# Four quarter products side by side in place of one float32 product of 128 weight columns

## The chip, the cores and the metric

The kernel runs on one core of a Trainium2 chip, as one launch. The metric is the device time of that core in microseconds. The kernel before takes 1728.89 us, the median of three runs (1727.22 to 1729.65).

## What is computed

Three layers run one after the other on 256 tokens of 1024 features, all in float32. Each layer is a mixer (products with large weights, around an attention or a recurrence) followed by a routed set of experts:

```
layer 0: forgetting attention + S5 scan    -> 16 experts of 256, two per token
layer 1: mLSTM, 8 heads of 128             -> 16 experts of 256, two per token
layer 2: sparse attention (8 heads of 128)
         + HGRN2 (8 heads of 128)
         + retention (4 heads, 256 x 512)  -> 32 experts of 512, two per token
```

Layer 2 scales and shifts its inputs by vectors worked out from a second input, `mod = silu(c) @ ada_w + ada_b`. The parts that the change touches are these:

```
s   = einsum('bhnld,bhnjd->bhnlj', qc, kc) * Dmat         # mLSTM scores; num = s @ v + ...
attn = einsum('bhtd,bhsd,bhtsd->bhts', qt, kt, decay)     # HGRN2
attn = einsum('bhtd,bhsd->bhts', qt, kt) * intra_decay    # retention; o = attn @ v + ...
logits = x @ w_group + b_group, x @ w_expert + b_expert   # both routers' kinds
```

## The kernel before, in words

Activations stand on the chip throughout. Weights come in pieces of 1 MB through a ring of tiles: `place` takes the next tile, `weights` (L246 to L261) issues the load on SP (L260). Where a list `after` is set, GpSimd first copies one value of a mark into the tile (L250), which holds the load back until an earlier piece was split; the marks are made in `split_now` (L279).

The large products of the mixers are made from halves. Each weight piece is split into a rounded part hi by ScalarE (L285) and a rest lo by VectorE (L286), and `mm3` issues three products (L301, L302, L303) of 128 weight columns and 256 streamed ones in a faster number format (float32r). These make up most of TensorE's work in the mixers. Everything else on TensorE is plain float32, which the engine does in two passes: one matmul of the program is one weight load and one product per pass, so two records of each in the trace.

Around the large products stand smaller float32 ones, and the names of their lines are used below:
- L565: the modulation for layer 2, done in small steps beside the mixers. Products with a streamed column of ones, four to each of 12 groups (4 groups in the second mixer, 8 in the third).
- L590: a vector spread over rows, with a diagonal tile as the streamed one.
- L956 to L958 (`attn_out`): scores by values, three products of 128 streamed columns to a head, for the mLSTM (sd and v), sparse attention (PT and av), HGRN2 (AT or AO and bi) and retention (AR and cv).
- L1199: the routers' logits, 8 products to each half of the tokens, 20 or 36 streamed columns; L1092 on VectorE reads them.
- L1537: scores of the mLSTM heads, an early half of 256 and a late half (t0 = 128) of 128 streamed columns.
- L1858 and L1853: HGRN2's levels. For each of seven levels in two halves VectorE makes qw (L1848), GpSimd fills in W (L1849, L1856), TensorE makes eight products of 64 streamed columns (L1858), and VectorE copies them into AT under a mask (L1861).
- L1923: retention's scores, again with an early and a late half.
- L872 and L906 belong to the S5 scan of layer 0. They are already issued with 32 weight columns at a column position of the array (`tile_position=(0, 32 * q)`), as are some of the experts' products in L1324. They are not changed.

The order of the instructions on each engine is written out ahead of the run: the framework simulates the program with its own costs and orders each engine's queue by it. A change in the number of instructions can so move others, on other engines too. Each engine works through its queue in order.

Of the kernel before, what the change touches and what calls it, by code (L numbers as in the profile page):

```python
# [200 lines left out]
class Net:  # L201
# [96 lines left out]
    def mm3(self, out, a, b, first, last):  # L298
# [3 lines left out]
        nc.tensor.matmul(out, a[0], b[1], start=False, stop=False)  # L302
        nc.tensor.matmul(out, a[1], b[0], start=False, stop=last)  # L303

    def dense_feat(self, hT, srcs, evac):


        c = 0
        q = None
        for src in srcs:  # L310
            w = self.weights(src)
            nk, n = w.shape[1], w.shape[2]
            step = min(n, 1024 // nk)
            for s0 in range(0, n, step):
                hi, lo = self.split(w[:, :, s0:s0 + step])
                for j in range(step // 128):
                    if q is None:
                        q = self.ps("z").rearrange("p (c t) -> p c t", c=2)
                    s = slice(128 * j, 128 * j + 128)
                    for k in range(nk):  # L320
                        self.mm3(q[:, c % 2, :], (hi[:, k, s], lo[:, k, s]), (hT[0][:, k, :], hT[1][:, k, :]), k == 0, k == nk - 1)
                    c += 1
                    if c % 2 == 0:
                        evac(c - 2, q)
                        q = None
        if q is not None:
            evac(c - 1, q)
# [190 lines left out]
    def v(self, name, n=128):  # L518

        at = VEC_AT[name]  # L520
        return self.vec[:n, at:at + dict(VEC)[name]]
# [23 lines left out]
    def modulation(self, p, js, every, bufs, after):  # L545


        nc, A, ct = self.nc, self.A, self.v("ct")
        def bits():
            for j in js:  # L550
                acc = p.tile([128, 512], F32, name="md")
                for k in range(8):
                    w = p.tile([128, 512], F32, name="aw", bufs=bufs)
                    if j == js[0] and k < bufs:
                        nc.gpsimd.tensor_copy(w[:, :1], after)
                    nc.sync.dma_start(w, A["aw"][j, k])
                    c = ct[:, k:k + 1]
                    if k:
                        nc.vector.scalar_tensor_tensor(acc, w, c, acc, op0=ALU.mult, op1=ALU.add)  # L559
                    else:  # L560
                        nc.vector.tensor_scalar(acc, w, c, None, op0=ALU.mult)
                    yield
                q = self.ps("a")
                for i in range(4):
                    nc.tensor.matmul(q[:, i:i + 1], acc[:, i * 128:(i + 1) * 128], self.ones[:, :1], start=True, stop=True)  # L565
                m = slice(4 * j, 4 * j + 4)
                nc.vector.tensor_add(self.modT[:, m], self.v("abT")[:, m], q[:, :4])
        self.beside, self.every, self.units = bits(), every, 0
# [12 lines left out]
    def rows(self, vec, tag):  # L581

        nc = self.nc
        out = []
        for n in range(2):
            q = self.ps(tag)
            for c in range(4):
                d = self.sm.tile([128, 128], F32, name="diag")
                nc.scalar.activation(d, self.ident, AF.Identity, scale=vec[:, 4 * n + c:4 * n + c + 1])
                nc.tensor.matmul(q[:, 128 * c:128 * c + 128], self.ones[:, :128], d, start=True, stop=True)  # L590
            out.append(q)
        return out

# [358 lines left out]

    def attn_out(self, a00, a01, a11, v, o):

        nc = self.nc
        nc.tensor.matmul(o[:, :128], v(0), a00, start=True, stop=True)  # L956
        nc.tensor.matmul(o[:, 128:256], v(0), a01, start=True, stop=False)  # L957
        nc.tensor.matmul(o[:, 128:256], v(1), a11, start=False, stop=True)  # L958

    def gate_in(self, p, hT, w, bias, name):  # L960

# [193 lines left out]
    def moe_core(self, l, x, gT, bT, add, end, po, first=None, last=None):  # L1155
# [4 lines left out]
        tc, nc, A = self.tc, self.nc, self.A  # L1160
# [13 lines left out]
        with self.phase(f"moe{l}", y=4, o=3, t=1) as p:  # L1174
            rw, rb = self.v(f"rw{l}").rearrange("p (k n) -> p k n", k=8), self.v(f"rb{l}")
# [3 lines left out]
            hT = xtile("mhT")  # L1179
            qs, rs, mr = [], [], []  # L1180
            for b in range(2):
                if l < 2:
                    mr.append(self.moments(x, b))
                    rs.append(mr[b][1])
                else:
                    rs.append(self.sm.tile([128, 1], F32, name="xrs"))
                    self.inv_rms_rows(x, b, rs[b], lambda c: hh[:, b, c * 512:(c + 1) * 512])
                for k in range(0, 8, 4):
                    v = self.ps("o").rearrange("p (k t) -> p k t", k=4)
                    for j in range(4):  # L1190
                        nc.tensor.transpose(v[:, j], x[:, b, 128 * (k + j):128 * (k + j) + 128], self.ident)
                    d = hT[:, k:k + 4, 128 * b:128 * b + 128]
                    if k:
                        nc.vector.tensor_copy(d, v)
                    else:
                        nc.scalar.activation(d, v, AF.Copy)
                qs.append(self.ps("y")[:, :rw.shape[2]])
                for k in range(8):
                    nc.tensor.matmul(qs[b], hT[:, k, 128 * b:128 * b + 128], rw[:, k, :], start=k == 0, stop=k == 7)  # L1199
            weigh, mk = self.route(p, l, ne, qs, rb, rs)  # L1200

            for b in range(2):
# [15 lines left out]
            q = self.ps("t")  # L1218
# [304 lines left out]
    def mlstm_heads(self, p, half, qT, kT, v, nm, aT):  # L1523

        nc = self.nc
        den = self.ps("n")
        num = self.late.tile([128, 4, 256], F32, name="num", bufs=2)
        r0 = 32 * half
        for i in range(4):
            hd = 4 * half + i  # L1530
            r = row_of(hd)
            d, s = self.ps("a"), self.ps("a")
            for o, t0 in ((0, 0), (256, 128)):
                n = 256 - t0
                nc.tensor.matmul(d[:, o:o + n], self.oh[:, hd, :], nm[:, t0:], start=True, stop=False)
                nc.tensor.matmul(d[:, o:o + 128], self.identb, self.cmtb, start=False, stop=True)
                nc.tensor.matmul(s[:, o:o + n], kT[:, i, t0:t0 + 128], qT[:, i, t0:], start=True, stop=True)  # L1537
            D = p.tile([128, 384], F32, name="Dm", bufs=2)
            nc.scalar.activation(D[:, :256], d[:, :256], AF.Exp, bias=aT[:, 0, r:r + 1])
            nc.scalar.activation(D[:, 256:], d[:, 256:384], AF.Exp, bias=aT[:, 1, r:r + 1])  # L1540
            sd = p.tile([128, 384], F32, name="sd", bufs=4)
            nc.vector.scalar_tensor_tensor(sd, s[:, :384], 128.0 ** -0.5, D, op0=ALU.mult, op1=ALU.mult)
            blocks = [sd[:, j * 128:(j + 1) * 128] for j in range(3)]
            o = self.ps("a")
            self.attn_out(*blocks, lambda kb: v[:, kb, i * 128:(i + 1) * 128], o[:, :256])
            nc.scalar.activation(num[:, i], o[:, :256], AF.Copy)
            m = r0 + 4
            oc = self.ones_column(r0 + i, m)
            nc.tensor.matmul(den[:m, :256], oc, sd[:, :256], start=i == 0, stop=False, skip_group_check=True)
            nc.tensor.matmul(den[:m, 128:256], oc, sd[:, 256:], start=False, stop=i == 3, skip_group_check=True)  # L1550
        return num, den
# [253 lines left out]
    def hgrn_weights(self, p, hT, half, e, lv):  # L1805

        nc = self.nc
# [26 lines left out]
        for i, m in enumerate((128, 64, 32, 16, 8, 4, 2, 1)):  # L1834
# [15 lines left out]
            s = self.ps("a")  # L1850
            if m == 128:
                for j in range(4):
                    nc.tensor.matmul(s[:, 128 * j:128 * j + 128], W[:, j, :128], qw[:, 128 * j:128 * j + 128], start=True, stop=True)  # L1853
                nc.scalar.activation(AO, s.rearrange("p (h t) -> p h t", h=4), AF.Copy)
                continue
            nc.gpsimd.tensor_copy(w1[:, :, :1], of(kk, m, 1)[:, :, :1])  # L1856
            for j in range(8):
                nc.tensor.matmul(s[:, 64 * j:64 * j + 64], W[:, j // 2, 128 * (j % 2):128 * (j % 2) + 128],  # L1858
                                 qw[:, 64 * j:64 * j + 64], start=True, stop=True)
            mk = lv[:, i - 1, :].bitcast(U16).rearrange("p (n s m) -> p n s m", s=2, m=m)[:, :, 1, :]  # L1860
            nc.vector.copy_predicated(AT.rearrange("p h b (n s m) -> p (h b) n s m", s=2, m=m)[:, :, :, 1, :],  # L1861
                                      mk.unsqueeze(1).to_broadcast([128, 8, 64 // m, m]),
# [35 lines left out]
    def retention_weights(self, p, hT, rot, half):  # L1898
# [20 lines left out]
        for h in range(2):  # L1919
            s = self.ps("a")  # L1920
            for o, t0 in ((0, 0), (256, 128)):
                for j in range(2):
                    nc.tensor.matmul(s[:, o:o + 256 - t0], ck[:, 2 * h + j, t0:t0 + 128], cq[:, 2 * h + j, t0:], start=j == 0, stop=j == 1)  # L1923
            nc.vector.tensor_tensor(AR[:, h], s[:, :384], dec[:, h], op=ALU.mult)
        return AR

# [78 lines left out]
```

## Time and profile before

| | |
|---|---|
| median of three runs | 1728.89 us |
| profiled execution | 1725.18 us |
| its span, first to last instruction | 1723.4 us |
| mean granted clock of TensorE | 0.913 |
| TensorE busy | 1491.4 us, 87% |
| VectorE / ScalarE / GpSimd busy | 851.5 / 615.5 / 258.1 us |
| HBM read | 467.56 MB |

The first mixer lies from 0 to 172 us, its experts up to 366; the second mixer from 366 to 490, its experts up to 650; the third mixer from 650 to about 1240, its experts to the end. In the profile PE is TensorE's products, PEld its weight loads, DVE VectorE, ACT ScalarE, POOL GpSimd, SP the queue that issues most transfers. The rows of stages give start and end, length, the busy time of PE, PEld, DVE, ACT and POOL with instruction counts, the granted clock, the busy share of the DMA engines and GB/s. The rows in order of time give start, length, engine, line and operation, tiles, shapes and a count where like instructions follow each other. A product's length in the profile reaches from its start to its modelled end, and products overlap; what one costs is therefore read from the distance between starts.

### The profile page before, as it was taken

The page shows a single profiled execution, that of the slowest core. Times are in us where ns is not written, and L with a number is a line of the kernel's source. Part 1 is how long each engine was busy: PE and PEld are TensorE (multiplying, and loading weights), DVE is VectorE, ACT ScalarE, POOL GpSimd, SP SyncE. Part 2 cuts the span into 40 slices and gives each one's busy share as a digit, 9 for nine tenths or more (in the row PEclk, how much of TensorE's full clock was granted, in tenths as well). Part 3 has the DMA queues.
Part 4 walks back from the last instruction along what each step waited for, and adds up shares of the span by engine and source line. Part 5 has one row for each costly group of instructions (what it writes and reads, how often), then busy time and mean ns, then how long its engine had stood idle before and what let it go on. Part 6 is the DMA issues. An engine that isn't in the chain of part 4 may idle for free.

```text
span 1723.4 us, 26173 instructions
## 1 busy us (share of the span) xinstructions
PE 1491.4 (87%) x10705; PEld 1058.6 (61%) x10705; DVE 851.5 (49%) x1411; ACT 615.5 (36%) x921; POOL 258.1 (15%) x290
## 2 busy tenths in 40 slices
PE   7889899799989978999999999999986766668664
PEld 6768544588864427999999999999830211113111
DVE  6665522677663236977887768567720000001002
ACT  4344311466531214557565455455510000002001
POOL 7840100000010001002214212225300000000000
PEclk9989999999989998999999999999987887777876
DMA  9714995665479916663464566444799999999996
GB/s 276 174 54 156 420 421 228 227 222 194 164 306 421 393 42 211 230 206 136 168 215 143 191 221 225 172 167 176 322 421 421 421 421 421 421 421 421 421 422 247
DMA packets 82266, 471.37 MB, mean 274 GB/s; under 512 B 12496, under 2 KB 14424, under 8 KB 29392
## 3 DMA queue, kind: packets, MB, share of 16 engines
q1 hardware_dynamic: 77920, 457.28, 68.2%
q0 software_dynamic: 2224, 8.85, 2.2%
q10 hardware_dynamic: 1984, 3.37, 0.8%
q8 instruction: 90, 1.47, 0.3%
q14 instruction: 48, 0.39, 0.1%
HBM read 467.56 MB, written 1.90 MB: 272 GB/s over the span
## 4 chain that ended last, share of the span: by engine, by line
PE 31%; DMA 25%; DVE 2%; ACT 1%; issue 1%; POOL 1%; POOLq 0%; SPq 0%; ACTq 0%; DVEq 0%
DMA w<-in_dn 9%; PE z L301 8%; PE z L302 8%; PE z L303 8%; DMA w<-in_g 8%; DMA w<-in_u 8%; PE a L1858 1%; PE o L1252 1%; DVE lo L286 1%; PE o L1324 1%; PE a L957 0%; PE a L958 0%; PE a L956 0%; DMA aw<-in_aw 0%; PE a L565 0%
## 5 line engine op out<-in xcount | busy, mean ns | idle before, releaser
L1324 PE MATMUL o<-w,xg 128*32 128x512 f32 (+1 forms) x1536 | 307.0, 740 | 90.1 <-DMA w<-in_u 46.0
L286 DVE TENSOR_TENSOR lo<-w,hi 128x1024 fp32r<-128x1024 f32 x243 | 317.1, 1309 | 102.4 <-ACT hi L285 82.8
L285 ACT ACTIVATE hi<-w 128x1024 fp32r<-128x1024 f32 x243 | 255.6, 1055 | 262.1 <-PE z L302 142.3
L301 PE MATMUL z<-hT,hi 128*128 128x256 f32 x1016 | 287.4, 284 | 5.8 <-DVE cv L1505 3.7
L303 PE MATMUL z<-hT,lo 128*128 128x256 f32 x1016 | 287.1, 283 | 5.1 <-DVE lo L286 5.0
L302 PE MATMUL z<-hT,hi 128*128 128x256 f32 x1016 | 286.9, 283 | 0.1
L1324 PEld LDWEIGHTS o<-w,xg 128*32 128x32 f32 (+1 forms) x1536 | 60.6, 127 | 302.4 <-DMA w<-in_u 116.8
L301 PEld LDWEIGHTS z<-hT,hi 128*128 128x128 f32 x1016 | 192.8, 190 | 8.8 <-issue 5.1
L303 PEld LDWEIGHTS z<-hT,lo 128*128 128x128 f32 x1016 | 192.6, 190 | 6.6 <-DVE lo L286 6.1
L302 PEld LDWEIGHTS z<-hT,hi 128*128 128x128 f32 x1016 | 192.5, 190 | 1.7 <-issue 1.1
L1324 PE MATMUL o<-w,hidT 128*32 128x512 f32 (+1 forms) x768 | 137.6, 671 | 28.7 <-DMA w<-in_dn 18.2
L1344 DVE TENSOR_TENSOR sg<-sg,o 128x512 f32<-128x512 f32 x8 | 5.5, 687 | 279.0 <-PE o L1324 279.0
L1372 DVE SCALAR_TENSOR_TENSOR evl<-o,ws,evh 128x512 fp32r<-128x512 f32 x48 | 36.0, 750 | 130.0 <-ACT evh L1369 130.0
L1324 PEld LDWEIGHTS o<-w,hidT 128*32 128x32 f32 (+1 forms) x768 | 31.0, 126 | 102.9 <-issue 47.9
L301 PE MATMUL z<-hi,hT 128*128 128x256 f32 x320 | 89.8, 283 | 2.7 <-DVE cv L1505 2.7
L302 PE MATMUL z<-lo,hT 128*128 128x256 f32 x320 | 90.0, 282 | 0.0
L303 PE MATMUL z<-hi,hT 128*128 128x256 f32 x320 | 89.4, 280 | 0.0
L1369 ACT ACTIVATE evh<-o,ws 128x512 fp32r<-128x512 f32 x48 | 33.0, 687 | 150.0 <-PE o L1324 150.0
L1283 ACT ACTIVATE PT<-t 128x256 fp32r<-128x256 f32 x24 | 9.2, 383 | 204.9 <-PE t L1281 156.9
L559 DVE SCALAR_TENSOR_TENSOR md<-aw,vec,md 128x512 f32<-128x512 f32 x84 | 62.7, 746 | 34.2 <-DMA aw<-in_aw 33.1
L303 PE MATMUL z<-oT,lo 128*128 128x256 f32 x256 | 72.9, 285 | 0.0
L301 PE MATMUL z<-oT,hi 128*128 128x256 f32 x256 | 72.7, 284 | 0.0
(627 smaller groups left out, 2720.7 us busy)
## 6 DMA issues: line engine op xcount, KB each, us to landing
w<-in_dn SPq DMA_DIRECT2D x96, 1024.0 KB, 19.8
w<-in_wi SPq DMA_DIRECT2D x66, 1024.0 KB, 4.8
w<-in_gu SPq DMA_DIRECT2D x64, 1024.0 KB, 11.1
w<-in_g SPq DMA_DIRECT2D x64, 1024.0 KB, 19.8
w<-in_u SPq DMA_DIRECT2D x64, 1024.0 KB, 19.8
aw<-in_aw SPq DMA_DIRECT2D x96, 256.0 KB, 3.6
w<-in_ow SPq DMA_DIRECT2D x16, 1024.0 KB, 4.9
w<-in_ew SPq DMA_DIRECT2D x8, 1024.0 KB, 11.5
```

The costliest lines, as they stand in the source:

```text
L285: self.nc.scalar.activation(hi, v, AF.Copy)
L286: self.nc.vector.tensor_tensor(lo, v, hi.bitcast(F32), op=ALU.subtract)
L301: nc.tensor.matmul(out, a[0], b[0], start=first, stop=False)
L302: nc.tensor.matmul(out, a[0], b[1], start=False, stop=False)
L303: nc.tensor.matmul(out, a[1], b[0], start=False, stop=last)
L559: nc.vector.scalar_tensor_tensor(acc, w, c, acc, op0=ALU.mult, op1=ALU.add)
L1252: nc.tensor.matmul(q[:, j], s[:, b, ds], Pv[:, b], start=i == 0, stop=i == 3)
L1283: nc.scalar.activation(PT, q[:, :256], AF.Copy)
L1324: self.nc.tensor.matmul(o[C * e:C * e + C, :], lhs(k0, e), w[:, e, k, :], start=k0 == 0, stop=k0 == nk - 1, tile_position=(0, C * e), skip ...
L1369: i = nc.scalar.activation(hi, o, AF.Identity, scale=ws)
L1372: nc.vector.scalar_tensor_tensor(lo, o, ws, hi.bitcast(F32), op0=ALU.mult, op1=ALU.subtract)
L1858: nc.tensor.matmul(s[:, 64 * j:64 * j + 64], W[:, j // 2, 128 * (j % 2):128 * (j % 2) + 128], qw[:, 64 * j:64 * j + 64], start=True, stop= ...
```

## The change

A helper `mm4` issues one product as four, each with 32 of the 128 weight columns, at column positions 0, 32, 64 and 96 of the array, into the matching 32 partitions of the output. It takes the place of the plain product in the lines named above, where the streamed tile has at most 128 columns and the output has 128 partitions.

```
+    def mm4(self, out, a, b, start=True, stop=True):
+        for i in range(0, 128, 32):
+            self.nc.tensor.matmul(out[i:i + 32], a[:, i:i + 32], b, start=start, stop=stop, tile_position=(0, i), skip_group_check=True)
 # modulation
-                    nc.tensor.matmul(q[:, i:i + 1], acc[:, i * 128:(i + 1) * 128], self.ones[:, :1], start=True, stop=True)
+                    self.mm4(q[:, i:i + 1], acc[:, i * 128:(i + 1) * 128], self.ones[:, :1])
 # rows
-                nc.tensor.matmul(q[:, 128 * c:128 * c + 128], self.ones[:, :128], d, start=True, stop=True)
+                self.mm4(q[:, 128 * c:128 * c + 128], self.ones[:, :128], d)
 # attn_out
-        nc.tensor.matmul(o[:, :128], v(0), a00, start=True, stop=True)
+        mm = self.mm4 if o.shape[0] == 128 else self.nc.tensor.matmul
+        mm(o[:, :128], v(0), a00, start=True, stop=True)
...
 # router
-                    nc.tensor.matmul(qs[b], hT[:, k, 128 * b:128 * b + 128], rw[:, k, :], start=k == 0, stop=k == 7)
+                    self.mm4(qs[b], hT[:, k, 128 * b:128 * b + 128], rw[:, k, :], start=k == 0, stop=k == 7)
 # mlstm_heads
-                nc.tensor.matmul(s[:, o:o + n], kT[:, i, t0:t0 + 128], qT[:, i, t0:], start=True, stop=True)
+                if t0:
+                    self.mm4(s[:, o:o + n], kT[:, i, t0:t0 + 128], qT[:, i, t0:])
+                else:
+                    nc.tensor.matmul(s[:, o:o + n], kT[:, i, t0:t0 + 128], qT[:, i, t0:], start=True, stop=True)
 # hgrn_weights
-                    nc.tensor.matmul(s[:, 128 * j:128 * j + 128], W[:, j, :128], qw[:, 128 * j:128 * j + 128], start=True, stop=True)
+                    self.mm4(s[:, 128 * j:128 * j + 128], W[:, j, :128], qw[:, 128 * j:128 * j + 128])
...
-                nc.tensor.matmul(s[:, 64 * j:64 * j + 64], W[:, j // 2, 128 * (j % 2):128 * (j % 2) + 128],
-                                 qw[:, 64 * j:64 * j + 64], start=True, stop=True)
+                self.mm4(s[:, 64 * j:64 * j + 64], W[:, j // 2, 128 * (j % 2):128 * (j % 2) + 128], qw[:, 64 * j:64 * j + 64])
 # retention_weights
+                    mm = self.mm4 if t0 else nc.tensor.matmul
```

In all 112 products of L1858, 120 of `attn_out`, 48 of L565, 48 of L1199, 40 of L590 and 8 each of L1537, L1853 and L1923 become four. The lines shift: the helper's product is L308 after the change, L1537 becomes L1545, L1535 becomes L1540.

TensorE's queue in the second mixer, at the second head of the mLSTM; sd is the weighted scores, qk the query and key, nr and cb the terms of the decay. Before:

```order
L302 MATMUL z<-hT,hi 128x256
L956 MATMUL a<-sd,v 128x128
L957 MATMUL a<-sd,v 128x128
L1535 MATMUL a<-nr,oh 128x256
L1536 LDWEIGHTS cb
L1536 MATMUL a<-cb 128x128
L1537 MATMUL a<-qk_4045,qk_4199 128x256
L1535 MATMUL a<-nr,oh 128x128
L958 MATMUL a<-sd,v 128x128
L1536 LDWEIGHTS cb
L1536 MATMUL a<-cb 128x128
L1537 MATMUL a<-qk_4045,qk_4199 128x128
```

Here the three products of sd and v are split by those of the next head. After the change, at the same place:

```order
L302 MATMUL z<-hT,hi 128x256
L308 MATMUL a<-sd,v 32x128 x12
L1540 MATMUL a<-nr,oh 128x256
L1541 LDWEIGHTS cb
L1541 MATMUL a<-cb 128x128
L1545 MATMUL a<-qk_4093,qk_4247 128x256
L1540 MATMUL a<-nr,oh 128x128
L1541 LDWEIGHTS cb
L1541 MATMUL a<-cb 128x128
L308 MATMUL a<-qk_4093,qk_4247 32x128 x4
L303 MATMUL z<-hT,lo 128x256
```

Twelve quarters of sd and v stand together, and the four of the late qk stand between products of 128 columns.

SP's queue at the end of the third mixer, where the loads of the experts' weights (in_g, in_u) follow those of the last mixer weights (in_wo). Before:

```order
L260 DMA w<-in_wo 128x2048 [waits DMAHW6_49,DVE_49]
L260 DMA w<-in_g 128x2048 [waits Pool_49]
L260 DMA w<-in_g 128x2048 [waits DMASW6_49,DMASW5_49,DMASW7_49,DMASW0_49,Pool_49]
L260 DMA w<-in_g 128x2048 [waits Pool_49] x3
L260 DMA w<-in_g 128x2048 [waits DMAHW7_49,Pool_49]
```

The loads of in_g follow at once, and the first of in_u comes after eight of them. After the change:

```order
L260 DMA w<-in_wo 128x2048 [waits DMAHW6_49,DVE_49]
L260 DMA w<-in_u 128x2048 [waits DMAHW7_49,DVE_49]
L260 DMA w<-in_g 128x2048 [waits Pool_49]
L260 DMA w<-in_g 128x2048 [waits DMASW6_49,DMASW5_49,DMASW7_49,DMASW0_49,Pool_49]
L260 DMA w<-in_g 128x2048 [waits Pool_49] x3
```

One load of in_u, which waits for VectorE, has moved ahead of those of in_g.

GpSimd's queue at the same place, with the marks (L279) and the copies that hold loads back (L250). Before:

```order
L1601 TENSOR_TENSOR merged<-merged,mg 128x512 [waits DVE_49,Pool_49]
L250 COPY w<-mark 128x1 [waits DMAHW7_49,PE_49]
L250 COPY w<-mark 128x1 [waits DMASW7_49,DMASW6_49,DMASW0_49]
L250 COPY w<-mark 128x1 x2
L250 COPY w<-mark 128x1 [waits DMAHW4_49,DMAHW5_49,DMAHW3_49,DMAHW6_49,DMAHW2_49,DMAHW7_49,DMAHW1_49,DMAHW0_49]
```

The copies follow the last addition directly. After the change:

```order
L1609 TENSOR_TENSOR merged<-merged,mg 128x512 [waits DVE_49,Pool_49]
L279 COPY mark<-lo 128x1 [waits DVE_49] x2
L250 COPY w<-mark 128x1 [waits DMAHW7_49,PE_49]
L250 COPY w<-mark 128x1 [waits DMASW7_49,DMASW6_49,DMASW0_49]
L250 COPY w<-mark 128x1 x2
```

Two marks, each of which waits for VectorE's lo, now stand between the addition and the copies.

## Rows read from the trace of the kernel before

**Rows 1.** Busy time by stage: second mixer, third mixer, last experts.
```profile
366.00:490.00 124.00, 120.32 (x873) 109.73 (x872) 88.81 (x130) 74.20 (x110) 0.00 (x0) 0.99 0.61 220
...
700.00:1222.00 522.00, 518.12 (x4357) 510.35 (x4357) 396.85 (x493) 293.98 (x368) 135.86 (x119) 1.00 0.53 187
...
1250.00:1705.00 455.00, 317.65 (x1817) 79.27 (x1816) 42.62 (x112) 35.92 (x73) 0.00 (x0) 0.78 1.01 419
```

**Rows 2.** TensorE's waits, 366 to 490 and 660 to 1222: total, times, longest.
```profile
PE z L301 <- DVE cv L1505: 3.3, 2, 2.7
...
PE z L303 <- DVE lo L286: 4.3, 2, 2.8
PE a L1858 <- POOL W L1856: 1.6, 3, 0.8
```

**Rows 3.** The chain that ended last, one of its pieces: start, length.
```profile
1276.19 19.81 DMA w<-in_g
```

**Rows 4.** Weight loads in order of time, at a block of L1858.
```profile
802.38 1.87 PEld L1858 LDWEIGHTS a<-qw,W 128*128 128x128 f32 x16
804.16 0.19 PEld L303 LDWEIGHTS z<-hT,lo 128*128 128x128 f32 x1
```

**Rows 5.** Products in order of time, at the same block.
```profile
802.49 1.89 PE L1858 MATMUL a<-qw,W 128*128 128x64 f32 x16
804.19 0.36 PE L303 MATMUL z<-hT,lo 128*128 128x256 f32 x1
804.39 0.28 PE L301 MATMUL z<-hT,hi 128*128 128x256 f32 x1
```

**Rows 6.** Line L565, its weight loads: shortest, median and longest in ns.
```profile
L565 PEld LDWEIGHTS a<-ones,md x96: 186/192/192, 364.4 to 1101.2; 128*128 128x128 f32 x96
```

**Rows 7.** Products in order of time, with 32 weight columns, four side by side.
```profile
117.47 1.26 PE L906 MATMUL y<-H,cl 128*32 128x31 f32 x126
118.56 0.36 PE L875 MATMUL s<-cl,bt 128*32 128x224 f32 x1
...
1260.67 13.94 PE L1324 MATMUL o<-w,xg 128*32 128x512 f32 x128
```

**Rows 8.** Products in order of time, where L872 stands between full products.
```profile
35.65 0.28 PE L302 MATMUL z<-hTl,hi 128*128 128x256 f32 x1
35.76 0.28 PE L303 MATMUL z<-hTh,lo 128*128 128x256 f32 x1
35.97 0.30 PE L872 MATMUL s<-cc,bt 128*32 128x16 f32 x4
36.20 0.38 PE L301 MATMUL z<-hTh,hi 128*128 128x256 f32 x1
36.42 0.28 PE L302 MATMUL z<-hTl,hi 128*128 128x256 f32 x1
```

**Rows 9.** Line L1858: idle time before it, and who waited for it (us, times).
```profile
  POOL W L1856: 3.9, 6
...
  DVE AT L1861: 5.5, 6
```

**Rows 10.** SP's issues in order of time, the first expert loads.
```profile
1222.58 4.69 SPq L260 DMA_DIRECT2D w<-in_g  x8
```

**Rows 11.** VectorE in order of time, its first reads of two routers' logits.
```profile
178.51 0.24 DVE L1092 SCALAR_TENSOR_TENSOR lg<-y,lrs,vec 128x20 f32<-128x20 f32 x1 [0.41 <-PE y L1199]
...
497.63 0.24 DVE L1092 SCALAR_TENSOR_TENSOR lg<-y,lrs,vec 128x20 f32<-128x20 f32 x1 [0.40 <-PE y L1199]
```

**Rows 12.** VectorE and GpSimd in order of time, around 1222 us.
```profile
1221.37 3.45 POOL L250 COPY w<-mark 128x1 f32<-128x1 f32 x7
...
1223.07 1.22 DVE L286 TENSOR_TENSOR lo<-w,hi 128x1024 fp32r<-128x1024 f32 x1
```

**Rows 13.** Busy time by stage, just ahead of the expert stream.
```profile
1222.00:1225.00 3.00, 3.00 (x17) 2.54 (x16) 2.30 (x3) 2.25 (x6) 2.94 (x9) 1.00 0.71 265
```

More of the change, by code (lines that the diff above doesn't have):

```diff
@@ L953, in attn_out @@
     def attn_out(self, a00, a01, a11, v, o):
-        nc = self.nc
-        nc.tensor.matmul(o[:, :128], v(0), a00, start=True, stop=True)
-        nc.tensor.matmul(o[:, 128:256], v(0), a01, start=True, stop=False)
-        nc.tensor.matmul(o[:, 128:256], v(1), a11, start=False, stop=True)
+        mm = self.mm4 if o.shape[0] == 128 else self.nc.tensor.matmul
+        mm(o[:, :128], v(0), a00, start=True, stop=True)
+        mm(o[:, 128:256], v(0), a01, start=True, stop=False)
+        mm(o[:, 128:256], v(1), a11, start=False, stop=True)
     def gate_in(self, p, hT, w, bias, name):
@@ L1922, in retention_weights @@
                 for j in range(2):
-                    nc.tensor.matmul(s[:, o:o + 256 - t0], ck[:, 2 * h + j, t0:t0 + 128], cq[:, 2 * h + j, t0:], start=j == 0, stop=j == 1)
+                    mm = self.mm4 if t0 else nc.tensor.matmul
+                    mm(s[:, o:o + 256 - t0], ck[:, 2 * h + j, t0:t0 + 128], cq[:, 2 * h + j, t0:], start=j == 0, stop=j == 1)
             nc.vector.tensor_tensor(AR[:, h], s[:, :384], dec[:, h], op=ALU.mult)
```

## The prediction, made before the run

> **What bounds the kernel now.** I read the stages first [rows 1]. In the second mixer (366 to 490 us) TensorE is busy 120.3 of 124 us and in the third (700 to 1222 us) 518.1 of 522, at a granted clock of 0.99 to 1.00; the DMA engines are used to 0.61 and 0.53 there. From 1250 to 1705 us the picture is turned round: TensorE is busy 318 of 455 us and the DMA share is 1.01 at 419 GB/s. Next come TensorE's waits [rows 2]: the longest of the second mixer come to 3.3 us, those of the third to 4.3 and 1.6. So time taken from or put on TensorE in the two mixers moves what follows almost one for one. Last the chain [rows 3]: from 1264 us on it is nearly all expert weights arriving, one piece of 19.8 us after another. What happens there on TensorE is hidden. The last stage ends a fixed stretch after its stream of weights starts, which SP's first load of in_g at 1222.58 us [rows 10] marks. **The time after is therefore the time before plus the shift of that start**, and every term below is a term of that shift (positive is faster).
>
> **What a product of the changed kind costs.** A float32 product is one instruction and two passes in the trace. Sixteen passes with 128 weight columns and 64 streamed ones: first weight load at 802.38, the next line's at 804.16, so 111 ns a pass [rows 4]; the weight load sets this, not the 64 columns. L565, with one streamed column, has the same loads of 192 ns [rows 6], of which the next product hides a part, and I give it the same 111; so too with 128 columns.
>
> Four products of 32 weight columns side by side: L906, with 31 streamed columns, runs 126 passes from 117.47 to 118.56 us, 8.7 ns each, so 35 ns for a set of four [rows 7]. L1324, with 512 columns, runs 128 passes in 13.94 us, 436 ns a set, 0.85 ns a column [rows 7]. The trace has no such set with 64 or 128 columns. By the rate per column alone they take 55 and 109 ns, by a line through both rows 62 and 116. I take 59 for 64 columns, and 111 (no change) for 128, since both ends lie within 5 ns of it; for 1 to 36 columns 35.
>
> The Trainium skill says otherwise of the loads: "TensorEngine Tiling (Array Packing)", Restrictions, has column tiling switch off the fast weight load. The trace does not bear out a loss from it: four loads and four products of 32 columns fit in 35 ns in L906 against 111 for one load of 128. If it cost anything here, the forecast would move to the serial rival below.
>
> **What going in and out of it costs.** Neighbours on TensorE are products of 128 weight columns, so each group of quarters is a change of array shape and a change back. A change inside a dense stretch stands at 35.76 us [rows 8]: from L303 there to L302 at 36.42 is 0.66 us, with L301, L872's four passes and nothing else between. Normal starts lie 0.11 us apart, two of these are 0.23, and four short passes 0.13 to 0.14. That leaves 0.30 us that a pair of changes costs. L872 starts 0.21 us after L303 began instead of 0.11, and L301 lasts 0.38 instead of 0.28 us before the next can follow, so on both sides something lies open that is hidden elsewhere. Bounds: 0.20 if half of the exit is already paid by the float32 block's own exit (804.19 to 804.39, 0.20 us, where starts lie 0.11 apart elsewhere [rows 5]), 0.43 if L872's passes are free. I keep 0.30, which is a measured row.
>
> The skill has the rule behind it: "TensorEngine Tiling (Array Packing)", Key Properties, says that a change of tiling mode, not of tile, drains TensorE. The row agrees and gives it a price; without the drain the sum below would be 17 us better.
>
> **The sum over TensorE.** Counted in the order listings, changes of shape rise from 64 to 105 between the first and second router and from 66 to 144 up to the third. Without those around the routers themselves this is some 18.5 more pairs in the second mixer and 38 in the third.
>
> - Second mixer: 16 products of L565 at 2 x (111 - 35) = 0.152 us give 2.4; L1537's late half (8), attn_out (24) and L590 (16) have 128 columns and give nothing. 18.5 pairs cost 5.6. Net -3.2 us. The first two listings of the change show why: L1537's quarter group stands alone between full products, and where the scores of sd and v were split around L1535 they now stand together.
> - Third mixer: 112 products of L1858 at 2 x (111 - 59) = 0.104 give 11.6 (10.8 to 12.5), 32 of L565 give 4.9; attn_out (96), L1923, L1853 and L590 (8 each) nothing. 38 pairs cost 11.4. Net +5.1 us. A block of eight L1858 alone is worth 8 x 0.104 - 0.30 = 0.53 us, there are 14.
> - Not all of that arrives. L1858 already waits for POOL's copy W (L1856), 3.9 us in 6 waits with its loads, and on the other side DVE's AT waits 5.5 us, 6 times, for L1858 [rows 9]. A quicker block frees DVE sooner, which frees qw and then W, so part of that loop gains too; where POOL sets the step, the gain becomes a wait. Between 0 and all 14 x 0.53 = 7.4 us; I take 1.5, three of 14 blocks, since L1858's row among TensorE's waits counts three [rows 2].
> - Routers: 16 products each of 20 columns save 2.4 us of TensorE, less a pair; but the next link is DVE's lg, which waits 0.41 and 0.40 us for them in the first two [rows 11], and TensorE's other work there is done. I take these 0.8 us (0 to 2). The third router at 1244 us lies under the saturated stream and counts nothing; so do L590 in the expert stage and all that follows.
> - The start of the stream. In SP's listing one load of in_u now stands before the eight of in_g, and waits for DVE. Queued behind it are all loads of in_g, which in the kernel before waited only for POOL's copies from 1221.37 us on [rows 12]. The DVE result that its slot waits for is the half ending at 1224.29 us, and POOL's two marks of that tile now stand ahead of its seven copies [rows 10, 12]. So the first in_g goes 1224.3 instead of 1222.58: -1.7 us. Nothing covers it: the DMA share is only 0.71 from 1222 to 1225 us [rows 13]. If DVE gets there early, or the missing stretch is made up by the in_u load already under way, it is 0.
>
> Sum: -3.2 + 5.1 - 1.5 + 0.8 - 1.7 = -0.5 us, slower by 0.5. The profiled execution took 1725.18 us (1.8 beside its span of 1723.4), so 1725.7 by it; the median of the runs, 1728.89, is 3.7 above it, so **1729.4 us**. Less than 0.2% (3.5 us) either way can't be told from no change here.
>
> **Rivals.**
> 1. Changes are cheaper than that row, half hidden (0.15 us). [...] Against it: the entry follows an L301 to L303 of 256 columns in nearly all places, as in [rows 8]. 56.5 x 0.15 = 8.5 us better: 1720.9.
> 2. Slower: the steps of the level recursion around L1858 are set by POOL's copy W, so TensorE comes early to every level and waits; the whole 7.4 us goes instead of 1.5. For it: the waits are on W already. Against it: DVE's waits for L1858 are longer than TensorE's for W. It decides from about 9 of the 14 blocks on, 4.8 us, which is 3.3 more than I took and brings the shift to 3.8; at all 14 the time is 1729.4 + 5.9 = 1735.3.
> 3. The change doesn't do what it says: the four quarters run one after the other. Then a block's pass costs 4 x 55 ns instead of 111, and of 128 columns 4 x 109: 112 x 2 x 0.11 = 24 us and in the mixers some 168 x 2 x 0.33 = 111 us worse, 1860. L906's 8.7 ns a pass speaks against it.
>
> **How the numbers follow.** Forecast 0.45, rival 1 0.25, rival 2 0.26, rival 3 0.02, anything else 0.02. The forecast's own range by the bounds of the routers, the stream's start and 64 columns is 1726 to 1733. The range 1721 to 1737 takes in rivals 1 and 2 and leaves out what is beyond them. Of the forecast most lies within 0.2%, a little on either side; rival 1 and 2 give faster and slower. Faster 0.28, same 0.42, slower 0.30.
>
> **What would show it.** In the profile after: a block of L1858 between two weight loads of its neighbours takes some 1.2 to 1.3 us instead of 1.78 (0.94 of it the passes); an L1537 quarter group costs 0.5 us where it cost 0.22; the second mixer's window grows by 3 us and the third's shrinks by 3 to 4; SP's first in_g comes behind an in_u that waits on DVE. If the second mixer does not grow, the price of a change is wrong. If TensorE's waits for W grow by several us, rival 2. If the third mixer shrinks by more than 8 us, rival 1. If the last stage's length from SP's first in_g to the end is not about 500 us, the claim that only its start counts is wrong.

## The result, and the profile after

| | before | after |
|---|---|---|
| median | 1729.27 us (4 runs) | 1739.65 us (4 runs) |
| profiled execution | 1725.18 us | 1737.16 us |
| its span | 1723.4 us | 1735.4 us |
| PE busy | 1491.4 us | 1486.5 us |

The ratio is 1.0064, 95% interval 1.0049 to 1.008: the change makes the kernel 10.4 us slower. Forecast were 1729.4 us and a range up to 1737; both are wrong, and so was the likeliest case of no measurable change.

First the stages, the two mixers with their ends moved along with the work, which answers to [rows 1]. The columns are those of [rows 1].

```profile
370.70:496.90 126.20, 121.38 (x1221) 105.06 (x1221) 87.42 (x126) 71.04 (x105) 0.00 (x0) 0.99 0.58 211
705.20:1230.80 525.60, 513.78 (x5912) 494.80 (x5911) 400.86 (x492) 293.55 (x366) 134.55 (x118) 1.00 0.53 186
1261.00:1716.00 455.00, 317.50 (x1913) 78.12 (x1911) 40.03 (x88) 35.05 (x68) 0.00 (x0) 0.78 1.01 419
```

The third mixer is 3.6 us longer although TensorE is busy 4.3 us less in it: what was taken off TensorE came back as waiting. The second mixer grew by 2.2 us. The last experts run on the same DMA share and rate as before.

The mm3 products (L301 to L303) number 5544 in both kernels, so the n-th of one can be set beside the n-th of the other, and the difference of their starts is the delay at that place. Other events that both have serve in the same way:

```
place (start in the kernel before)                 delay after, us
end of the first mixer, product 528    (166.9)      1.22
first read of the experts' result, L1439 (316.3)    2.88
start of the second mixer, product 600 (335.2)      4.69
end of the second mixer, product 1440  (486.1)      6.86
start of the third mixer, product 1480 (658.4)      6.24
before the levels, product 2400        (790.6)      5.25
after the levels, product 3500         (967.6)      4.89
end of the mixer, product 5400        (1211.7)      8.78
first in_g on SP                      (1222.6)     10.93
end of the span                       (1723.4)     11.98
```

The 1.22 us at the first place mean nothing: kernels of the experiments below whose code is that of the kernel before up to there stand between -0.25 and 4.7. The other 10.8 us are the loss in this pair of profiles.

Now the price of a group, as the products follow each other in time (columns as in [rows 5]). A block of L1858 in the changed kernel, which answers to [rows 5]:

```profile
806.53 0.28 PE L301 MATMUL z<-hT,hi 128*128 128x256 f32 x1
806.74 1.10 PE L308 MATMUL a<-qw,W 128*32 128x64 f32 x64
807.77 0.38 PE L302 MATMUL z<-hT,hi 128*128 128x256 f32 x1
807.99 0.28 PE L303 MATMUL z<-hT,lo 128*128 128x256 f32 x1
```

From the last full product to the second one behind, 1.46 us; in the kernel before the same stretch took 2.02 (0.12 ahead of 802.49, then to 804.39). The gain is 0.56 us, forecast 0.53. The quarters do run side by side: 64 passes in 1.03 us, and from set to set their starts lie 56 ns apart, where I took 59. A group of L565 in the changed kernel:

```profile
1013.66 0.28 PE L303 MATMUL z<-oT,lo 128*128 128x256 f32 x1
1013.87 0.43 PE L308 MATMUL a<-ones,md 128*32 128x1 f32 x32
1014.24 0.39 PE L301 MATMUL z<-hi,hT 128*128 128x256 f32 x1
1014.46 0.28 PE L302 MATMUL z<-lo,hT 128*128 128x256 f32 x1
```

In the same measure 0.80 us, against 1.13 before (1008.42 to 1009.55): a gain of 0.33, forecast 0.31.

Products with 128 streamed columns, retention's scores by values in the changed kernel:

```profile
1027.18 0.28 PE L302 MATMUL z<-hT,hi 128*128 128x256 f32 x1
1027.38 2.85 PE L308 MATMUL a<-AR,cv 128*32 128x128 f32 x96
1030.17 0.39 PE L303 MATMUL z<-hT,lo 128*128 128x256 f32 x1
1030.39 0.28 PE L301 MATMUL z<-hT,hi 128*128 128x256 f32 x1
```

The measure is 3.21 us from 1027.18 to 1030.39, less two normal starts 2.97. Twenty-four full passes at 111 ns are 2.66, so as quarters this group costs 0.31 us more than that. (In the kernel before it stood as two groups of 8 and 16 passes, 1021.80 to 1022.93 and 1023.16 to 1025.19, which come to 2.71 in the same measure.) Its sets start 110 ns apart: the pair of shape changes buys nothing.

With the sets and two normal starts taken off, a pair of changes costs 0.33 us in the first of these groups, 0.31 in the second and 0.33 in the third, with 64, 1 and 128 streamed columns.

TensorE's waits in the levels of the third mixer, total, times and longest, of the changed kernel, which answer to [rows 2]:

```profile
PE a L308 <- POOL W L1864: 5.8, 7, 1.5
PE z L303 <- DVE lo L286: 3.6, 3, 1.7
PE a L308 <- DVE qw L1856: 0.7, 1, 0.7
```

L1864 is L1856 of before. It was waited for 1.6 us and is now waited for 5.8.

SP's issues at the start of the expert stream, which answer to [rows 10]:

```profile
1233.13 0.33 SPq L260 DMA_DIRECT2D w<-in_u  x1
1233.51 5.26 SPq L260 DMA_DIRECT2D w<-in_g  x8
1240.76 16.39 SPq L260 DMA_DIRECT2D w<-in_u  x7
```

The moved in_u holds in_g back: the delay grows by 2.15 us between the mixer's last products and in_g (8.78 to 10.93).

### The profile page after: what moved, and what is told of

The parts are those of the page before. It is cut to its first block, busy times and chain, and to the rows that moved or that the text cites. A ratio compares the mean times of both kernels' runs of the same rounds, so it can differ in the third digit from the quotient of the medians.

```text
span 1735.4 us, 30902 instructions
## 1 busy us (share of the span) xinstructions
PE 1486.5 (86%) x13057; PEld 1033.2 (60%) x13057; DVE 858.0 (49%) x1411; ACT 613.5 (35%) x919; POOL 255.3 (15%) x290
## 5 line engine op out<-in xcount | busy, mean ns | idle before, releaser
L301 PE MATMUL z<-hT,hi 128*128 128x256 f32 x1016 | 288.3, 284 | 3.7 <-ACT hT L285 1.9
L303 PE MATMUL z<-hT,lo 128*128 128x256 f32 x1016 | 287.0, 283 | 4.6 <-DVE lo L286 4.4
L301 PEld LDWEIGHTS z<-hT,hi 128*128 128x128 f32 x1016 | 192.7, 190 | 8.3 <-issue 4.4
L303 PEld LDWEIGHTS z<-hT,lo 128*128 128x128 f32 x1016 | 192.3, 189 | 7.9 <-DVE lo L286 6.0
L301 PE MATMUL z<-hi,hT 128*128 128x256 f32 x320 | 90.2, 283 | 3.2 <-DVE cv L1510 3.2
L303 PE MATMUL z<-hi,hT 128*128 128x256 f32 x320 | 89.7, 281 | 0.0
L303 PE MATMUL z<-oT,lo 128*128 128x256 f32 x256 | 72.9, 285 | 1.6 <-DVE lo L286 1.6
L301 PE MATMUL z<-oT,hi 128*128 128x256 f32 x256 | 72.7, 284 | 0.0
```

The source lines that it names most:

```text
L301: nc.tensor.matmul(out, a[0], b[0], start=first, stop=False)
```

## The experiments

Each experiment is the kernel before with some lines of the change, or with an edit of its own; the kernel before ran in the same session. "Blocks" below is TensorE's time in everything but mm3, "waits" its idle time before an instruction, both summed between the same mm3 products in the two traces.

**Only 128 streamed columns.**

```
+ L590, attn_out, L1537, L1853, L1923 as in the change
  L1858, L565, L1199 as in the kernel before
```

> Only the products with 128 streamed columns as quarters (L590, attn_out, L1537, L1853, L1923); the rest as before. Theory P (a pair of shape changes costs 0.30 us, a pass of four quarters with 128 columns 116 ns instead of 111): 18 pairs in the second mixer 5.4 us and some 20 in the third 6.0 us, longer passes 1.7 us, and in_u ahead of in_g again 2 us: 13 to 15 us slower than before, more than the whole change. Rival O (only the reordered queues cost): 3 to 5 us slower.

Measured: 1741.88 us against 1728.16, ratio 1.0096 (1.0073 to 1.0118), 13.7 us slower. From product 600 to 5400 the delay grows by 9.5 us, 2.1 more at in_g. The blocks are 9.8 us longer there and the waits 0.8 (the pace of the mm3 products gives 1.1 back), so price P holds and rival O is out: these products pay for the pairs and get nothing. This part alone costs as much as the whole change; whether more can't be told, since the two intervals overlap.

**Only 64 streamed columns or fewer.**

```
+ L1858, L565, L1199 as in the change
  the rest as in the kernel before
```

> Only the products with 64 or fewer streamed columns as quarters (L1858, L565, L1199); the rest as before. Theory P with levels that are set by GpSimd and VectorE: L565 gives 12 chunks x 0.33 = 4 us, L1858 and the routers about 1 us: 4 to 6 us faster than before; TensorE's waits at L1858 for W and qw rise from 1.6 us to about 6. Rival T (TensorE sets the levels' pace, so all 14 x 0.56 us arrive): 11 to 13 us faster, waits unchanged. Rival O: within 3 us of before.

Measured: 1727.24 us against 1728.16, ratio 0.9999 (0.9987 to 1.0011). In the levels the blocks give 8.5 us and the waits take 5.7 back. Of the 4 to 6 us that P allowed, 2.4 are lost ahead of that, from the end of the first mixer to the start of the second, where only the router is changed.

**Only L1858.**

```
+ L1858 as in the change
  the rest as in the kernel before
```

> Only L1858 as quarters. Each block shorter by 0.56 us on TensorE, 14 blocks 7.8 us. Theory P with levels set by GpSimd and VectorE: 0 to 2.5 us faster, and waits at L1858 up by 5 to 6 us. Rival T: 7 to 8 us faster.

Measured: 1727.64 us, ratio 0.9993 (0.9982 to 1.0004). TensorE's waits between 790 and 975 us:

```profile
PE a L308 <- POOL W L1861: 5.1, 8, 1.6
PE z L303 <- DVE lo L286: 3.5, 4, 1.5
```

Between products 2400 and 3500 the blocks fall by 7.7 us, the waits grow by 5.9, and the stretch is 1.4 us shorter. Rival T is out; three quarters of the gain are turned into waits.

**Only L565.**

```
+ L565 as in the change
  the rest as in the kernel before
```

> Only L565 as quarters: 12 chunks of four products, each 0.33 us shorter with its pair of shape changes included. Theory P: 3 to 4 us faster (1.3 in the second mixer, 2.6 in the third). Rival (a small group of quarters costs more than it gives): slower by 2 to 4 us.

Measured: 1733.54 us, ratio 1.0029 (1.0019 to 1.004), 5.4 us slower, against both expectations in size or sign. Half of it, 2.7 us, is lost in the second mixer, and not through the groups. TensorE's waits in its last part:

```profile
PE a L1571 <- DVE rr L295: 2.4, 1, 2.4
PE z L301 <- DVE cv L1510: 2.2, 1, 2.2
```

L1571 (L1566 of before) starts the last step of the heads. In this kernel the last head's scores stand later in TensorE's queue, so that step comes late and VectorE's rr later still; before, TensorE did not wait for rr at all. Right behind this wait the granted clock of TensorE is 0.50 (1.2 GHz) from 477.8 to 481.0 us, where the kernel before stays at 1.00 (2.4 GHz). The delay first falls from 3.51 us at product 600 to 0.03 at product 1200 and then runs up to 6.22 at product 1440. The third mixer adds 1.8 us: its blocks give 1.7, its waits take 2.5 and the pace of the mm3 products 0.9.

**The same, third mixer alone.**

```
+ if j < 4: the plain product        (the second mixer's four groups)
+ else:     self.mm4(...)            (the third mixer's eight)
```

> L565 as quarters only in the third mixer's eight groups; the four of the second mixer as in the kernel before. If what cost 5 us with all twelve was the order of the second mixer's queues: the second mixer as before (L1566's wait of 2.4 us gone), the third 2.6 us shorter by eight groups of 0.33: 1.5 to 3 us faster than before. If a small group of quarters itself costs: 2 to 4 us slower.

Measured: 1729.92 us, ratio 1.0012 (1.0001 to 1.0022). The second mixer is back as it was (0.06 us shorter, no wait for rr). So what it lost came with its four groups, and by the waits and the clock above it came through the order of its queue, not through the groups' own time. The 2.6 us of the third mixer do not come: the blocks give 2.1 there, and then the mm3 products run 2.2 us longer in its last part, without one more wait. That belongs to the last section. By its time this kernel lies where the rival, a group that itself costs, had it; the trace shows no such cost, but it also accounts for only 0.5 us of the slowdown from product 600 to the end, and the rest is open.

**The copy into W on VectorE**, in three kernels:

```
- nc.gpsimd.tensor_copy(w1[:, :, :1], of(kk, m, 1)[:, :, :1])
+ nc.vector.tensor_copy(w1[:, :, :1], of(kk, m, 1)[:, :, :1])
```

> The kernel before with the copy into W (L1856) on VectorE right behind qw, instead of GpSimd; no quarters. TensorE's waits for that copy were 1.6 us in the kernel before. Theory G (the levels' pace is set by the path over GpSimd's copy): 1 to 2 us faster. Theory V (VectorE itself sets the pace): 0 to 2 us slower, since VectorE has 14 more instructions of some 0.2 us.

Measured, with nothing else changed: 1727.2 us, ratio 0.9998 (0.999 to 1.0007). The wait falls from 1.6 to 0.6 us, the levels are 2.1 us shorter by the trace, and the time is the same.

> L1858 alone as quarters, and the copy into W on VectorE. Theory G: the 5.1 us that TensorE waited for W with L1858 as quarters mostly go; 4 to 6 us faster than L1858 as quarters alone (ratio to before 0.9965 to 0.997). Theory V: the waits go over to qw or stay, within 1.5 us of L1858 as quarters alone.

Measured, with L1858 as quarters: 1725.97 us, ratio 0.9987 (0.9977 to 0.9996). The waits:

```profile
PE a L308 <- DVE W L1861: 3.3, 5, 1.0
PE z L303 <- DVE lo L286: 1.5, 1, 1.5
```

The wait for W falls from 5.1 to 3.3 us, and the levels are 4.2 us shorter than before instead of 1.4. By time it can't be told from L1858 alone (about 1 us, and the intervals overlap).

> The whole change, with the copy into W on VectorE. Theory G (in the levels the gain of the shorter blocks turns into waits on the path over GpSimd's copy): the part of the third mixer around the levels gets 3 to 5 us shorter than in the changed kernel, the whole 3 to 5 us faster than it, still 5 to 8 us slower than before. If the levels did not matter: within 1 us of the changed kernel.

Measured, with the whole change: 1739.59 us, ratio 1.0068 (1.0055 to 1.0081), no gain. The wait for W does fall, from 5.8 to 3.3 us, but the one for lo grows from 3.6 to 5.7:

```profile
PE z L303 <- DVE lo L286: 5.7, 4, 2.2
PE a L308 <- DVE W L1864: 3.3, 5, 1.2
```

The three together: the path over GpSimd's copy is a part of what the levels wait for, but not all. With the copy gone from it, TensorE waits for VectorE's lo and qw. Theory G holds for the waits for W alone. By its time the second kernel came out as theory V had it, and the third as if the levels did not matter. What sets the pace in the changed kernel stays open.

**The parts that looked good together.**

```
+ L1858 as in the change, L565 for j >= 4 only, the copy into W on VectorE
```

> L1858 as quarters, L565 as quarters in the third mixer only, the copy into W on VectorE. By theory G 6 to 9 us faster than before, by theory V 2 to 4 us faster.

Measured: 1724.85 us against 1727.33, ratio 0.9986 (0.9975 to 0.9996): faster than the kernel before by 2.5 us, as theory V had it (2 to 4) and less than theory G. The levels' stretch is 8.0 us shorter by the trace, nearly what the blocks promised, with this left to wait from 790 to 975 us (the longer of the two waits for lo lies ahead of product 2400):

```profile
PE z L303 <- DVE lo L286: 2.9, 2, 1.5
PE a L308 <- DVE W L1864: 1.8, 4, 0.7
PE a L308 <- DVE qw L1856: 0.7, 1, 0.7
```

From product 600 to 5400 this trace is 6.4 us ahead, but the time only 2.5. The rest is not explained: with one profile to a kernel, a stage is not known to better than some us of time.

**Only the routers.**

```
+ L1199 as in the change
  the rest as in the kernel before
```

> Only the routers' L1199 as quarters. The forecast had 0.8 us of gain. By the traces of the changed kernel and of the one with the products up to 64 columns as quarters, which both lose 2.4 to 3.5 us between the first mixer's end and the second mixer's start: 2 to 3 us slower than before, and that in the first experts and the second mixer's start, through their queues. If that loss comes from something else: within 1 us.

Measured: 1732.4 us, ratio 1.003 (1.0017 to 1.0042), 4.9 us slower. The step itself gives a little: TensorE's next product behind the router, L1220, which waits for the routing, is 0.23 us less late than the last mm3 product of the mixer. But 1.4 us are lost from there to L1439 in the first experts, 1.6 up to the second mixer's start, 1.0 in the second mixer, 1.4 in the last part of the third. Only the first two were expected. The reason in the experts is seen in the order of products. The kernel before:

```profile
296.87 0.73 PE L1375 MATMUL y<-evh,PT 128*128 128x512 f32 x2
297.44 0.63 PE L1375 MATMUL y<-evl,PT 128*128 128x512 f32 x2
298.00 1.94 PE L1324 MATMUL o<-w,xg 128*64 128x512 f32 x8
...
303.71 0.44 PE L1360 MATMUL t<-cst,sg 128*128 128x128 f32 x2
```

The routers' kernel:

```profile
299.60 0.73 PE L1380 MATMUL y<-evh,PT 128*128 128x512 f32 x2
...
300.73 1.07 PE L1329 MATMUL o<-w,xg 128*64 128x512 f32 x2
301.73 0.74 PE L1380 MATMUL y<-evh,PT 128*128 128x512 f32 x2
302.39 1.93 PE L1329 MATMUL o<-w,xg 128*64 128x512 f32 x6
...
307.64 0.44 PE L1365 MATMUL t<-cst,sg 128*128 128x128 f32 x2
```

Eight products of 64 columns were one group; now a full product stands between two and six of them. From L1375 to L1360 it was 6.84 us and is 8.04. The changed kernel has the same order there and the same 1.2 us.

The 1.6 us at the second mixer's start are the clock. Its first mm3 products, in the kernel before and in the routers' kernel (columns as in [rows 1]):

```profile
329.00:333.00 4.00, 3.87 (x30) 3.67 (x31) 3.75 (x7) 2.86 (x5) 0.01 (x1) 1.00 1.00 383
```

```profile
332.90:336.90 4.00, 3.96 (x18) 3.95 (x19) 3.73 (x7) 2.87 (x5) 0.00 (x0) 0.50 0.97 387
```

In both, TensorE has stood idle for 7.0 us shortly ahead, and the granted clock fell to half (0.50, 1.2 GHz) in that time. In the kernel before it is back at 1.00 (2.4 GHz) when these products start, and they start 117 ns apart; in the routers' kernel they run at half for 4 us, 213 ns apart. So it is in all five kernels with the routers as quarters, and in none of the other eight. Why the clock comes back later in them is not shown.

**The change without L590.**

```
- self.mm4(q[:, 128 * c:128 * c + 128], self.ones[:, :128], d)
+ nc.tensor.matmul(q[:, 128 * c:128 * c + 128], self.ones[:, :128], d, start=True, stop=True)
```

> The whole change without L590. In SP's queue the first in_u is then back behind in_g. Theory: the stream of expert weights starts with the same shift as the last products of the mixer, so 2.1 us are gained there, and 1.5 to 2 us by seven pairs of shape changes that fall away: 3.5 to 4.5 us faster than the changed kernel. If the place of in_u does not matter: 1.5 to 2 us.

Measured: 1738.26 us, ratio 1.0069 (1.0053 to 1.0085), not told apart from the change itself. What it was to show, it shows: in_u is back behind in_g,

```profile
1234.28 4.67 SPq L260 DMA_DIRECT2D w<-in_g  x8
1239.20 19.09 SPq L260 DMA_DIRECT2D w<-in_u  x8
```

and in_g is delayed by 11.70 us, as are the last products (11.70), so the 2.15 us are gone. But the second mixer got 1.4 us longer than in the changed kernel, and the stretch before the levels 1.4, which takes it back. In the second mixer the clock has a part again: TensorE is granted 0.50 from 364.1 to 367.3 us and from 432.3 to 439.0, in the changed kernel only from 432.4 to 435.6. In all kernels with in_g first the delay of in_g is that of product 5400 within 0.1 us; in the three with in_u first it is 2.1 us more.

## Why the prediction was wrong, by its own steps

Two terms failed. Of the gain in the levels the prediction took 1.5 us to be lost in waits; 7.2 us came off TensorE's blocks there, 7.6 came back as waits, and the stretch got 0.4 shorter. And the routers, which it took for a gain of 0.8 us, lost 3.5.

- **The price of a group: right.** 0.56 us for a block of L1858 (0.53 forecast), 0.33 for a group of L565 (0.31), 0.31 lost by a group of 128 columns (0.30). The sets take 32, 56 and 110 ns with 1, 64 and 128 columns (35, 59 and 111). A pair of changes costs 0.31 to 0.33 us whatever the columns, so rival 1, half that price, is out; and the quarters run side by side, so rival 3 is.
- **The sum over TensorE: right within 1.1 us.** Second mixer -3.2 us forecast; between products 600 and 1440 the blocks are 2.1 us longer. That the stretch is too, 2.2, is luck: 1.15 us more of waits meet 1.06 given back by the pace of the mm3 products. The granted clock is at 0.50 there in one place in the changed kernel (432.4 to 435.6 us) and in two in the kernel before (358.3 to 361.5 and 426.5 to 429.7). Third mixer +5.1 forecast; its blocks give 0.0 before the levels, 7.2 in them and -1.4 behind, together 5.8.
- **"Not all of that arrives ... I take 1.5": wrong in size.** Between products 2400 and 3500 the waits grew by 7.6 us: 4.8 on W and qw, 1.9 on lo, 0.6 on md. The blocks got 7.2 us shorter, the stretch only 0.4. That is rival 2 at its end, all 14 blocks, in size, and its sign came, the wait for W up from 1.6 to 5.8 us; its reason, GpSimd's copy, is only a part of it, since the whole change with the copy on VectorE was no faster. I had read DVE's waits for L1858 (5.5 us, [rows 9]) as a sign that a quicker block would speed up the loop. Only one of 1.1 us is left, and TensorE waits instead.
- **Routers, 0.8 us of gain: wrong in sign.** From the first mixer's end to the second mixer's start 3.5 us are lost, and the kernel with the routers alone loses 2.8 there. I reckoned with the wait of L1092 and left out that its quarters let the framework reorder the experts' queue behind it (1.2 us), and that the clock could then be at half when the second mixer starts (1.8 us in the changed kernel).
- **The start of the stream, 1.7 us: right**, 2.15 measured, and shown by the three kernels with in_u first against the ten without.
- **That only its start counts:** nearly. From in_g to the end, the span grew by 1.05 us more; in kernels with nothing changed behind in_g it is 0.0 to 0.7. It is in the stream itself: the last in_dn is issued 10.6 us later but lands 11.9 later, and the end is 12.0 later. Why it takes longer was not looked into. That piece of the chain before and after:

```profile
1685.30 19.79 DMA w<-in_dn
```

```profile
1695.87 21.16 DMA w<-in_dn
```

- **Not in the sum at all:** the pace of the mm3 products in the third mixer (the last section), 2.5 us lost behind the levels and 1.2 won in and before them.

Together: 3.5 + 2.2 - 0.6 - 1.0 - 0.4 + 3.9 + 2.15 + 1.05 = 10.8 us from the first mixer's end on, by the steps of the table above. Of the forecast's rivals the second, at its price of 5.9 us, had the right place and only part of the reason, and its time of 1735.3 us lacks what the routers cost.

## What to carry to other kernels

Price a group by the stretch between its neighbours, with the change of array shape in it: here that price, 0.30 us a pair, said rightly what each kind of group gives or costs on TensorE, though not what the kernel's time would do: L565 gains by it, and both kernels with L565 alone were slower. Then ask for every microsecond saved on a busy engine who hands it its next input, because a loop over several engines gives back the gain as a wait. Where a framework orders the queues by its own costs, read the order of every stage, not only of the changed places: edits of a few products moved others by 2 to 5 us either way. And compare the granted clock stretch by stretch before a difference is put down to the order of a queue.

## What was not expected of the hardware

Mm3 products of equal shape run at one of two paces, a median of 113 or 118 ns from start to start, at the full granted clock, and in most places keep it until something else comes between (at product 4680, where the tiles change roles from z<-hT,hi to z<-hi,hT, it goes from 118 to 113 ns with nothing between, in the kernel before and in the changed one). The same 11 us of mm3 products behind L565's group at 1008.54 us: the kernel before, the kernel with L565 changed in the third mixer alone, and the changed kernel.

```profile
1010.00:1021.00 11.00, 11.00 (x99) 11.00 (x98) 8.68 (x10) 4.27 (x5) 0.86 (x1) 1.00 0.80 286
```

```profile
1010.20:1021.20 11.00, 11.00 (x96) 11.00 (x95) 8.79 (x12) 4.10 (x5) 1.53 (x1) 1.00 0.77 279
```

```profile
1014.60:1025.60 11.00, 11.00 (x96) 11.00 (x95) 8.83 (x12) 4.11 (x5) 1.53 (x1) 1.00 0.76 279
```

TensorE has the granted clock 1.00 in all three, is busy throughout, and starts fewer products where the group ahead was one of quarters. At this place and at the next L565 group, 38 us later, all seven kernels with L565 as quarters there run at 118 ns and all six without at 113 (the changed kernel and the one before counted with the eleven). Behind retention's third group (product 4800) it is the four kernels with attn_out as quarters against the nine without. So here leaving the quarters went with another 4 to 5 ns a product for as long as mm3 ran undisturbed, 110, 110 and 49 products: 0.2 to 0.5 us, about as much as a pair. It is no rule: at product 1830 three of the seven kernels with quarters in the group ahead run at 113 and the kernel before at 118, and at product 5010 kernels whose queue is the same there have either pace. Why leaving a group sets it was not tried.

The first mixer takes up to 5 us more or less from one profile to the next with the same code (the delays at product 528 lie between -0.25 and 4.7), which is why stages were compared from there on.
